# A two-block transformer kernel: the second block's head groups projected one ahead, masks and rotations on VectorE, meta rows padded

## The chip, the cores and the metric

The kernel runs on one core of one Trainium2 chip. The metric is the device time of one execution in microseconds (us); less is better. The core's engines are named as in the profile: PE is TensorE's matmul, PEld its weight load, DVE VectorE, ACT ScalarE, POOL GpSimd, SP SyncE, which issues most DMAs.

## The reference, cut to what matters

Two transformer blocks run one after the other on 256 tokens of width 1024, all in float32. The change touches only the mixer of the second block. It prepends 16 meta tokens (so 272 keys), and computes two attentions from one projection:

```python
u = rms_norm(h, pre_mix_gain)
qa, ka, va, qb, kb, vb, g = split(u @ w_in)   # qa: 16 heads of 64, ka/va: 4; qb/kb: 8 heads x 2 x 64; vb: 8 x 128
qa, ka, qb, kb = rope(...)
# windowed: key within +-128 positions, all meta keys, and a sink logit without a value
s = concat([where(mask, qa @ ka.T / 8, -1e30), qa @ ka_meta.T / 8, sink])
o_swa = softmax(s)[:, :-1] @ concat([va, va_meta])
# differential: dense over all 272 keys
o_diff = rms_norm((softmax(q1 k1) - lam * softmax(q2 k2)) @ vb) * gain
merged = sigmoid(g1) * (o_swa @ w_swa) + sigmoid(g2) * (o_diff @ w_diff)
```

## The kernel before

All weights are one stream of 128x1024 units (`next_unit`, L321; `fetch`, L287): SP fetches a unit by DMA (`raw`), ACT rounds it to fp32r (`hi`, two casts of 512 columns, L302), DVE forms the remainder (`lo`, two subtractions, L304). A float32 product is three fp32r matmuls (hi hi, hi lo, lo hi), so that one unit gives 24 matmuls of 256 or 272 columns (`mm_a`, L459). PE works through the units in stream order.

The mixer of the second block (from L924, 398 to 689 us of the trace with its neighbours) first projects values and the keys `ka`. The loop over `c` (four groups of four heads) projects the queries of its group (`q_ps`, two units), rotates them (`rope_T`, L492: ACT copies `raw` out of PSUM, tile name `t` in the profile; four DMAs on ACT's queue swap halves; DVE multiplies by the cosine, L512; `self.slow` multiplies by the sine, L513, and adds, L516), and stacks high and low parts (`stack_q`, L519: ACT rounds, `self.slow` subtracts, L526 and L527). `self.slow` is POOL here. Then `sink_attention` (L599) is called for two tiles of 128 queries (`qt`): for each of four heads a score tile in PSUM (two matmuls, and a third that adds the mask as a bf16 identity product, L566), and `sink_softmax`: DVE writes the sink logit into the score tile (L577) and takes the minimum (L571), ACT takes the exponential with its sum (L581), DVE the reciprocal (L583) and the scaling (L584). PE transposes the probabilities (`pt_ps`, L620), ACT and DVE split them into `pt` (L330, L331), and PE multiplies by the values (`o_ps`, L624); the third key tile is the 16 meta keys, and its matmuls contract over 16 rows. The first block uses `sink_softmax1` instead, with the mask and minimum in one DVE instruction.

The loop over `pr` (four pairs of differential heads) projects keys and queries of its pair, and for each head: scores, softmax, the difference `a` (L1013), its transposes (`at_ps`, `atm_ps`), and `od_ps`: for each `qt` two matmuls over 128 keys (L1032, L1033) and one over the 16 meta keys (L1034). Behind it comes a norm: ACT squares (`y`, L1038), DVE `ms` (L1040), POOL a power (`rq`, L1042), DVE scales (`y`, L1044), PE transposes (`ot_ps`, L1048), ACT and DVE split into `od_t`. The gates (`gate_ps`) and the two branch projections (`bs_ps` from `os_t`, `bd_ps` from `od_t`) follow.

The order of each engine is not that of the source: a scheduler picks among the instructions whose inputs it thinks ready, by priority, and puts projections between the steps of the attention. PSUM has few banks: projections (`acc`) rotate over two, the score tiles over three while the windowed attention runs, and `o_ps`/`od_ps` have one. A projection's bank comes free when ACT has copied it out.

## Time and profile before

| | |
|---|---|
| median of 3 runs | 908.08 us (905.95 to 909.29) |
| profiled execution | 907.98 us |
| its span, first to last instruction | 906.2 us |
| mean granted clock of TensorE | 0.994 of full speed |
| PE busy | 885.2 us, 98% of the span |
| DVE, ACT, POOL busy | 69%, 58%, 17% |
| the mixer's stretch, 398 to 689 us | PE busy 285.73 of 291 us |

The span is what the trace holds; 1.8 us of the execution's time lie outside of it. An engine's busy time counts the time in which at least one of its instructions runs. Matmuls overlap: one takes longer than the distance to the next one's start, so costs on PE are read from starts.

### The profile page before, as it was taken

How to read it: one execution, taken by the hardware profiler on the slowest of the kernel's cores; microseconds unless marked ns; L12 is line 12 of the kernel's file. 1: busy time of each engine (PE TensorE's matmuls, PEld its weight loads, DVE VectorE, ACT ScalarE, POOL GpSimd, SP SyncE). 2: the span in 40 equal slices, each digit the busy share in tenths (PEclk: the TensorE clock that was granted, in tenths of full speed). 3: DMA queues.
4: the chain of work that ended last, by engine and by line, in shares of the span. 5: the costliest groups of instructions: out<-in, count | busy, mean ns of one | idle time of the engine just before them, and what ended most of it. 6: DMA issues, size and time to landing. Idle time of an engine off the chain costs nothing. (4 is left out here: it accounts for less than half of the span.)

```text
span 906.2 us, 16452 instructions
## 1 busy us (share of the span) xinstructions
PE 885.2 (98%) x6172; PEld 814.2 (90%) x6172; DVE 626.4 (69%) x1203; ACT 522.1 (58%) x1145; POOL 150.4 (17%) x171
## 2 busy tenths in 40 slices
PE   6999999999999999999989999999999999999997
PEld 5899999998899999978978889899998799999996
DVE  5567698768655555665699999987566675656654
ACT  4643389546654444565658788876455554444542
POOL 2001110110001111110464535450110100000000
PEclk9999999999999999999989999999999999999999
DMA  8665754468476666654654344434467566666651
GB/s 296 223 204 178 200 165 149 151 206 310 163 215 197 187 190 186 204 192 153 179 171 113 110 119 132 133 91 135 140 186 237 183 216 202 187 186 187 187 162 46
DMA packets 48320, 160.25 MB, mean 177 GB/s; under 512 B 6497, under 2 KB 8417, under 8 KB 48242
## 3 DMA queue, kind: packets, MB, share of 16 engines
q1 hardware_dynamic: 43378, 153.49, 54.2%
q10 hardware_dynamic: 4672, 5.20, 2.1%
q8 instruction: 48, 0.79, 0.4%
q0 software_dynamic: 192, 0.52, 0.2%
q14 instruction: 30, 0.25, 0.1%
HBM read 151.38 MB, written 2.10 MB: 169 GB/s over the span
## 5 line engine op out<-in xcount | busy, mean ns | idle before, releaser
L304 DVE TENSOR_TENSOR lo<-raw,hi 128x512 fp32r<-128x512 f32 x536 | 373.7, 738 | 187.1 <-ACT hi L302 182.0
L302 ACT CAST hi<-raw 128x512 fp32r<-128x512 f32 x532 | 302.0, 618 | 231.3 <-issue 81.7
L471 PE MATMUL op<-hi,hid 128*128 128x512 f32 x416 | 128.9, 390 | 0.0
L459 PE MATMUL fi_ps<-xf2t,hi 128*128 128x256 f32 x640 | 114.4, 281 | 0.0
L459 PEld LDWEIGHTS fi_ps<-xf2t,hi 128*128 128x128 f32 x640 | 99.0, 188 | 0.9
L459 PE MATMUL fi_ps<-xf2t,lo 128*128 128x256 f32 x320 | 90.1, 281 | 0.0
L471 PEld LDWEIGHTS op<-hi,hid 128*128 128x128 f32 x416 | 76.3, 188 | 14.7
L471 PE MATMUL op<-lo,hid 128*128 128x512 f32 x208 | 81.1, 392 | 0.0
L459 PE MATMUL f_ps<-xf1t,hi 128*128 128x256 f32 x448 | 80.5, 281 | 0.0
L459 PEld LDWEIGHTS f_ps<-xf1t,hi 128*128 128x128 f32 x448 | 69.9, 188 | 1.2
L459 PE MATMUL f_ps<-xf1t,lo 128*128 128x256 f32 x224 | 63.0, 281 | 0.0
L459 PEld LDWEIGHTS fi_ps<-xf2t,lo 128*128 128x128 f32 x320 | 60.6, 189 | 0.0
L459 PE MATMUL q_ps<-x2t,hi 128*128 128x256 f32 x256 | 52.0, 294 | 0.0
L459 PE MATMUL gate_ps<-x2t,hi 128*128 128x256 f32 x256 | 48.7, 285 | 0.0
L459 PE MATMUL gate_ps<-x1t,hi 128*128 128x256 f32 x256 | 47.1, 283 | 0.0
L471 PEld LDWEIGHTS op<-lo,hid 128*128 128x128 f32 x208 | 39.0, 188 | 8.6
L459 PEld LDWEIGHTS q_ps<-x2t,hi 128*128 128x128 f32 x256 | 41.9, 195 | 0.8 <-issue 0.5
L459 PEld LDWEIGHTS f_ps<-xf1t,lo 128*128 128x128 f32 x224 | 42.4, 189 | 0.1
L853 POOL TENSOR_TENSOR sq<-relu 128x512 f32<-128x512 f32 x14 | 15.9, 1133 | 150.4 <-ACT relu L850 150.4
L459 PEld LDWEIGHTS gate_ps<-x2t,hi 128*128 128x128 f32 x256 | 39.9, 189 | 0.6 <-issue 0.5
L459 PEld LDWEIGHTS gate_ps<-x1t,hi 128*128 128x128 f32 x256 | 39.6, 189 | 0.2
L419 POOL TENSOR_SCALAR e<-ss 128x1 f32<-128x1 f32 (+1 forms) x11 | 3.0, 276 | 220.4 <-ACT py L1087 191.9
(321 smaller groups left out, 2004.0 us busy)
## 6 DMA issues: line engine op xcount, KB each, us to landing
raw<-in_wstream_dram SPq DMA_DIRECT2D x272, 512.0 KB, 4.1
sw<-t ACTq DMA_DIRECT2D x40, 64.0 KB, 4.1
x<-in_x_dram SPq DMA_DIRECT2D x3, 512.0 KB, 5.9
sw<-t ACTq DMA_DIRECT2D x40, 34.0 KB, 2.5
sw<-t ACTq DMA_DIRECT2D x8, 128.0 KB, 3.7
g_pre<-in_gains_dram SPq DMA_DIRECT2D x2, 512.0 KB, 6.5
x<-hf SPq DMA_DIRECT2D x2, 512.0 KB, 2.6
x<-x SPq DMA_DIRECT2D x2, 512.0 KB, 7.4
```

The lines of the kernel that those rows point to most:

```text
L302: nc.scalar.copy(hi[:, c:c + PIECE], raw[:, c:c + PIECE])
L304: nc.vector.tensor_sub(lo[:, c:c + PIECE], raw[:, c:c + PIECE], hi[:, c:c + PIECE].bitcast(F32))
L419: nc.gpsimd.tensor_scalar(out=e[:np_], in0=ss[:np_, 0:1], scalar1=1.0 / D, scalar2=EPS, op0=ALU.mult, op1=ALU.add)
L459: nc.tensor.matmul(out, wv[a][:, k, j * P:(j + 1) * P], XT[:, b, k, n0:n1], start=(i == 0), stop=(i == last))
L471: nc.tensor.matmul(out, XT[:, b, k0 + k, t0:t1], wv[a][:, k, c0:c0 + cn], start=(start and i == 0), stop=(stop and i == last))
L853: nc.gpsimd.tensor_tensor(out=q, in0=r, in1=r, op=ALU.mult)
```

## The change

Six edits in the second block, with the order of the weight stream changed to match:

- The queries of group `c + 1` are projected before the attention of group `c`; in the last group the first pair's keys and queries; the same for the pairs.
- `self.slow` is no longer POOL in this block: rotation and low query parts run on DVE.
- The mask matmuls are gone. A float32 table `masks2` (128 x 544) holds both masks; one DVE instruction reads the score tile, adds the mask, and takes the minimum with the sink, as in the first block. It writes to SBUF (`pn`); the exponential runs in place there, and the scaling is a copy with a scale on ACT. POOL copies the sink column.
- The output tile is combined through two ACT copies of 64x256 (first block's form) instead of one of 64x512.
- `vm` and two `atm` tiles have 128 rows, zero but for 16, so that `od_ps`'s third matmul contracts over 128 rows. `o_ps`'s meta matmuls still contract over 16.
- `ks` and `kl` have eight buffers instead of six; the value copies `vt` use `kl`'s.

```diff
-    "b2": dict(vt=4, sw=2, t1=2, t2=2, ks=6, kl=6, qe=2, qo=2, p=6, a=2, at=1, atm=2, y=1, pn=2, pt=2),
+    "b2": dict(sw=2, t1=2, t2=2, ks=8, kl=8, qe=2, qo=2, p=6, a=2, at=1, atm=2, y=1, pn=2, pt=2),
...
-    def scores(self, out, q, k, k0, k1, mask=None):
+    def scores(self, out, q, k, k0, k1):
...
-        nc.tensor.matmul(out, q, k[1][:, k0:k1], start=False, stop=(mask is None))
-        for i, (mi, c0) in enumerate(mask or ()):
-            nc.tensor.matmul(out[:, c0:c0 + P], self.identb, self.masks[:, mi * P:(mi + 1) * P],
-                             start=False, stop=(i == len(mask) - 1))
+        nc.tensor.matmul(out, q, k[1][:, k0:k1], start=False, stop=True)
...
-    def sink_softmax(self, s, n, nsink, out):
-
-        nc = self.nc
-        nc.vector.tensor_copy(s[:, n:n + 1], nsink)
-        nm = self.row_min(s)
-        p = self.t([P, NKEY + 2], "p")
-        den = self.sm(1, "den")
-        nc.scalar.activation(out=p[:, :n + 1], in_=s, func=AF.Exp, bias=nm, scale=-1.0, accum_out=den)
-        rc = self.sm(1, "rc")
-        nc.vector.reciprocal(rc, den)
-        nc.vector.tensor_scalar(out=out, in0=p[:, :n], scalar1=rc, scalar2=None, op0=ALU.mult)
-
-    def sink_softmax1(self, s, n, mask, nsink, p):
+    def sink_softmax(self, s, n, mask, nsink, p):
...
-        if isinstance(masks, list):
-            pn = self.t([P, 4, n], "pn")
...
+        pn = self.t([P, 4, n + 1], "pn")
+        nc.gpsimd.tensor_copy(pn[:, :, n], sink[:, 4 * c:4 * c + 4])
+        for h in range(4):
+            s = self.sbank([P, n], "s")
+            self.scores(s, q[h % 2][:, h // 2, qt * P:(qt + 1) * P], kst, 0, n)
+            self.sink_softmax(s, n, mask, sink[:, 4 * c + h:4 * c + h + 1], pn[:, h, :])
...
-        self.slow = nc.gpsimd
         rope_b = self.load("rope_b", [P, 2 * NKEY])
+        mk = self.load("masks2", [P, 2 * NKEY], rp)
...
-        vm = self.t([NMETA, D], "vm")
+
+        vm = self.t([P, D], "vm")
+        nc.gpsimd.memset(vm, 0.0)
+        atms = [self.t([P, NTOK], "atm") for _ in range(2)]
+        for t in atms:
+            nc.gpsimd.memset(t, 0.0)
...
+        qn = queries()
         for c in range(4):
-            q = self.stack_q(self.rope_T(self.proj_a(XT, name="q_ps"), 2, NTOK, rope_b, 32, scale=-0.125))
+
+            q = qn
+            if c < 3:
+                qn = queries()
+            else:
+                kn = keys()
+                qn = queries()
...
         for pr in range(4):
-            kb = keys()
-            q = self.stack_q(self.rope_T(self.proj_a(XT, name="q_ps"), 2, NTOK, rope_b, 32, scale=-0.125))
+            kb, q = kn, qn
+            if pr < 3:
+                kn = keys()
+                qn = queries()
...
-                atm = self.t([NMETA, NTOK], "atm")
-                nc.scalar.copy(atm, b[:NMETA])
+                atm = atms[m]
+                nc.scalar.copy(atm[:NMETA], b[:NMETA])
```

What the scheduler makes of it is seen in the engines' orders. A number behind a tile's name tells its instances apart; a row begins with the line, which is some lines off between the two kernels.

DVE ahead of the first score tile of the first group, before (`lo147` belongs to weight unit 147, and so on; `s_5080` is the first score tile):

```order
L304 TENSOR_TENSOR lo147_5861<-raw147_5862,hi147_5860 128x512 x2
L304 TENSOR_TENSOR lo148_5896<-raw148_5897,hi148_5895 128x512 x2
L304 TENSOR_TENSOR lo149_5949<-raw149_5950,hi149_5948 128x512 x2
L512 TENSOR_TENSOR t1_5591<-t2_5592,rope_b_4683 128x512
L304 TENSOR_TENSOR lo150_5981<-raw150_5982,hi150_5980 128x512 x2
L577 COPY s_5080<-nsink_347 128x1
L577 COPY s_5106<-nsink_347 128x1
L571 TENSOR_REDUCE mn_5085<-s_5080 128x1
```

And the same place of the changed kernel, where `s_5164` is the first score tile, and `masks2` and `nsink` are read by the one instruction:

```order
L314 TENSOR_TENSOR lo147_5808<-raw147_5809,hi147_5807 128x512
L529 TENSOR_TENSOR qe_5074<-t1_5064,qe_5074 64x512
L530 TENSOR_TENSOR qo_5075<-t1_5064,qo_5075 64x512
L314 TENSOR_TENSOR lo148_5843<-raw148_5844,hi148_5842 128x512
L519 TENSOR_TENSOR t1_5146<-t1_5146,sw_5145 128x512
L314 TENSOR_TENSOR lo148_5843<-raw148_5844,hi148_5842 128x512
L314 TENSOR_TENSOR lo149_5878<-raw149_5879,hi149_5877 128x512
L515 TENSOR_TENSOR t1_5388<-t2_5389,rope_b_4677 128x512
L579 ISA pn_5162,mn_5167<-s_5164,masks2_4679,nsink_341 128x272
```

The first score tile's DVE work stood behind unit 150's remainder and stands behind unit 149's now; the query's low parts (`qe`, `qo`) and sine steps (L519), which POOL held, stand among the remainders.

PE of the changed kernel at the end of the stretch in which the last two groups' attention runs. `s_6522` and `s_6529` are scores of the first differential head, `o_ps_5768` the second tile of group 2, `q_ps_6838` the queries of the second pair:

```order
L605 MATMUL o_ps_5768<-pt_5774,va_4798 128x512 x2
L605 MATMUL o_ps_5768<-pt_5784,va_4798 128x512 x2
L566 MATMUL s_6522<-ks_6014,qo_6153 128x272
L567 MATMUL s_6522<-kl_6015,qo_6153 128x272
L933 MATMUL vT_ps_5952<-ident_93,vt_5839 128x128
L933 MATMUL vT_ps_5952<-ident_93,vt_5874 128x128
L933 MATMUL vT_ps_5952<-ident_93,vt_5909 128x128
L933 MATMUL vT_ps_5952<-ident_93,vt_5944 128x128
L566 MATMUL s_6529<-ks_6008,qe_6152 128x272
L567 MATMUL s_6529<-kl_6009,qe_6152 128x272
L605 MATMUL o_ps_5768<-pt_5794,va_4798 128x512
L462 MATMUL q_ps_6838<-x2t_2567,hi162_6783 128x256 x2
```

ACT of the changed kernel for the same stretch (`pn_6238` are the probabilities of group 3's second tile; `pt_5794` goes into the last `o_ps_5768` above; the copy of `k_ps_6726` frees the bank that `q_ps_6838` takes):

```order
L582 ACTIVATE pn_6238,den_6265<-pn_6238,mn_6263 128x273
L340 CAST os_t_4884<-of_5719 128x2x128
L585 ACTIVATE pn_6238<-pn_6238,rc_6247 128x272
L972 COPY vm_4682<-vT_ps_5946 16x512
L582 ACTIVATE pn_6238,den_6275<-pn_6238,mn_6273 128x273
L585 ACTIVATE pn_6238<-pn_6238,rc_6257 128x272
L990 ACTIVATE p_6520,den0_6513<-s_6515,mn_6518 128x272
L585 ACTIVATE pn_6238<-pn_6238,rc_6267 128x272
L340 CAST pt_5794<-pt_ps_5789 16x512
L509 COPY t2_6761<-k_ps_6726 128x272
```

Scores, transposes and value products stand here without a projection between them on PE, and the next projection stands behind them; on ACT the copy that lets it begin is the last row.

PE before, behind the last differential head's `od_ps`, where the transposes of its normed output (`ot_ps_7776`) stand between gate projections, 38 matmuls of them behind `od_ps`:

```order
L459 MATMUL gate_ps_8118<-x2t_2573,lo183_8120 128x256
L459 MATMUL gate_ps_8118<-x2t_2573,hi183_8119 128x256 x2
L459 MATMUL gate_ps_8118<-x2t_2573,lo183_8120 128x256
L1048 MATMUL ot_ps_7776<-ident_93,y_7766 128x128
L459 MATMUL gate_ps_8118<-x2t_2573,hi183_8119 128x256
L1048 MATMUL ot_ps_7776<-ident_93,y_7766 128x128
L459 MATMUL gate_ps_8118<-x2t_2573,hi183_8119 128x256
L459 MATMUL gate_ps_8118<-x2t_2573,lo183_8120 128x256
```

And PE of the changed kernel at the last two heads (`od_ps_7664` is the last one, `ot_ps_7608` and `ot_ps_7681` the transposes of the last two heads' normed outputs):

```order
L462 MATMUL bd_ps_8090<-od_t_6318,hi184_8056 128x256 x2
L462 MATMUL bd_ps_8090<-od_t_6318,lo184_8057 128x256
L1040 MATMUL ot_ps_7608<-ident_93,y_7598 128x128 x2
L1024 MATMUL od_ps_7664<-vb_4681,at_7658 128x128
L1025 MATMUL od_ps_7664<-vb_4681,at_7658 128x128
L1026 MATMUL od_ps_7664<-vm_4682,atm_4685 128x128
L1024 MATMUL od_ps_7664<-vb_4681,at_7658 128x128
L1025 MATMUL od_ps_7664<-vb_4681,at_7658 128x128
L1026 MATMUL od_ps_7664<-vm_4682,atm_4685 128x128
L462 MATMUL bd_ps_8090<-od_t_6318,hi184_8056 128x256 x2
L462 MATMUL bd_ps_8090<-od_t_6318,lo184_8057 128x256
L1040 MATMUL ot_ps_7681<-ident_93,y_7671 128x128 x2
```

The gates stand ahead of these heads now, and three matmuls of `bd_ps` lie between the last `od_ps` and its `ot_ps`.

## Rows read from the trace of the kernel before

**Rows 1.** The page, part 1: each engine's busy us, share of the span, instructions.

```profile
PE 885.2 (98%) x6172; PEld 814.2 (90%) x6172; DVE 626.4 (69%) x1203; ACT 522.1 (58%) x1145; POOL 150.4 (17%) x171
```

**Rows 2.** Windows: stretch, length, busy us of PE, PEld, DVE, ACT, POOL; clock.

```profile
457.00:476.00 19.00, 15.91 (x100) 14.94 (x101) 17.52 (x34) 10.24 (x28) 10.29 (x7) 0.82 0.52 166
...
550.00:575.00 25.00, 24.86 (x192) 23.07 (x191) 23.44 (x46) 21.53 (x53) 13.54 (x13) 1.00 0.46 141
...
sum 291.00, PE 285.73 PEld 262.81 DVE 232.96 ACT 197.56 POOL 100.15; mean PE 25.98 PEld 23.89 DVE 21.18 ACT 17.96 POOL 9.10
```

**Rows 3.** Waits of PE from 398 to 689 us: total, times, longest.

```profile
PE s L563 <- ACT p L581: 2.9, 2, 2.2
```

**Rows 4.** Windows of two stretches in which PE idles.

```profile
105.00:115.00 10.00, 8.52 (x72) 8.31 (x71) 5.33 (x11) 4.38 (x9) 2.68 (x5) 1.00 0.90 224
468.80:475.70 6.90, 6.32 (x29) 6.08 (x30) 5.72 (x22) 4.09 (x14) 0.00 (x0) 0.51 0.58 183
```

**Rows 5.** PE's timeline, three places: start us, us, line, operation, count.

```profile
482.12 0.63 PE L624 MATMUL o_ps<-pt,va 128*128 128x512 f32 x2
482.58 0.60 PE L620 MATMUL pt_ps<-ident,pn 128*16 128x128 f32 x4
...
506.30 0.23 PE L566 MATMUL s<-masksb,identb 128*128 128x128 bf16 x1
506.33 0.48 PE L624 MATMUL o_ps<-pt,va 128*128 128x512 f32 x1
...
582.61 0.49 PE L1020 MATMUL at_ps<-ident,a 128*128 128x128 f32 x3
582.93 0.27 PE L1025 MATMUL atm_ps<-ident,a 128*16 128x128 f32 x1
...
583.29 0.38 PE L1032 MATMUL od_ps<-vb,at 128*128 128x128 f32 x2
...
584.88 0.48 PE L1034 MATMUL od_ps<-vm,atm 16*128 16x128 f32 x2
585.30 0.39 PE L564 MATMUL s<-kl,qe 128*128 128x272 f32 x1
585.53 0.29 PE L563 MATMUL s<-ks,qo 128*128 128x272 f32 x1
585.65 0.29 PE L564 MATMUL s<-kl,qo 128*128 128x272 f32 x1
```

**Rows 6.** The weights' lo subtraction, 398 to 689 us: ns least/median/most.

```profile
L304 DVE TENSOR_TENSOR lo<-raw,hi x136: 670/685/1819, 398.3 to 686.7; 128x512 fp32r<-128x512 f32 x136
```

**Rows 7.** Groups of instructions, 398 to 689 us: busy us, mean ns.

```profile
L304 DVE TENSOR_TENSOR lo<-raw,hi 128x512 fp32r<-128x512 f32 x136 | 110.0, 845 | 24.1 <-ACT hi L302 24.0
...
L584 DVE TENSOR_SCALAR pn<-p,rc 128x272 f32<-128x272 f32 x32 | 14.3, 476 | 0.2
...
L571 DVE TENSOR_REDUCE mn<-s 128x1 f32<-128x273 f32 x32 | 13.2, 429 | 0.1
```

**Rows 8.** Groups of the first block's attention: busy us, mean ns.

```profile
L597 ACT ACTIVATE pn<-pn,rc 128x256 f32<-128x256 f32 x8 | 3.9, 505 | 0.1
L591 DVE CUSTOM_DVE_ANT_0 pn<-s,masks,nsink 128x256 f32<-128x256 f32 x8 | 3.7, 479 | 0.0
...
L635 ACT COPY of<-o_ps 64x256 f32<-64x256 f32 x8 | 2.9, 369 | 1.6 <-PE o_ps L624 1.0 <-DVE of L636 0.5
```

**Rows 9.** ACT's timeline at 592 us: start us, us, line, operation.

```profile
592.40 0.49 ACT L998 ACTIVATE p<-s,mn 128x272 f32<-128x272 f32 x1
...
592.88 0.58 ACT L1022 COPY at<-at_ps 128x512 f32<-128x512 f32 x1
593.35 0.29 ACT L1038 ACTIVATE y<-od_ps 128x128 f32<-128x128 f32 x1
```

**Rows 10.** Timeline behind the last head's od_ps, 643 to 645.5 us.

```profile
643.08 0.28 ACT L1038 ACTIVATE y<-od_ps 128x128 f32<-128x128 f32 x1 [1.35 <-PE od_ps L1034]
...
644.71 0.61 DVE L1044 SCALAR_TENSOR_TENSOR y<-od_ps,rq,rows 128x128 f32<-128x128 f32 x2 [0.80 <-POOL rq L1042]
```

More of the change, by code (lines that the diff above doesn't have):

```diff
@@ L119, in pack_weights, with kq @@
     in_a(w_in2, o_ka)
+    def kq(p):
+        in_a(w_in2, o_kb + 256 * p)
+        in_a(w_in2, o_qb + 256 * p)
+    in_a(w_in2, o_qa)
     for c in range(4):
-        in_a(w_in2, o_qa + 256 * c)
+        if c < 3:
+            in_a(w_in2, o_qa + 256 * (c + 1))
+        else:
+            kq(0)
         if c == VB1:
@@ L183, in make_consts @@
     j = np.arange(P)[None, :]
-    add("masks", np.concatenate([np.where(j <= i, 0.0, MASKED), np.where(j >= i, 0.0, MASKED)], axis=1))
-    add("masks1", np.concatenate([np.where(j > i, 0.0, MASKED), np.where(j <= i, 0.0, MASKED)], axis=1))
+    le, ge, gt = (np.where(c, 0.0, MASKED) for c in (j <= i, j >= i, j > i))
+    z = np.zeros((P, P))
+    add("masks1", np.concatenate([gt, le], axis=1))
+    add("masks2", np.concatenate([z, le, z[:, :NMETA], ge, z, z[:, :NMETA]], axis=1))
     f = _freqs(500000.0, 16)
@@ L366, in consts2 @@
         cc = _CC
-        mk = self.wp.tile([P, UC], F32, tag="raw", bufs=4, name="mk")[:, 0:2 * P]
-        a, n = cc["masks"]
-        nc.sync.dma_start(out=mk, in_=io["consts"][:, a:a + n])
-        self.identb = cp.tile([P, P], BF16, name="identb")
-        self.masks = cp.tile([P, 2 * P], BF16, name="masksb")
-        nc.gpsimd.tensor_copy(self.identb, self.ident)
-        nc.gpsimd.tensor_copy(self.masks, mk)
         self.vec = cp.tile([P, 48], F32, name="vec")
@@ L597, in sink_softmax1, with sink_attention @@
         nc.scalar.activation(out=p[:, :n], in_=p[:, :n], func=AF.Copy, scale=rc)
-    def sink_attention(self, q, kst, vs, sink, ktiles, masks, OT, c, qt):
+    def sink_attention(self, q, kst, vs, sink, ktiles, mask, OT, c, qt):
         nc = self.nc
         n = ktiles[-1][0] + ktiles[-1][1]
-        if isinstance(masks, list):
-            pn = self.t([P, 4, n], "pn")
-            for h in range(4):
-                s = self.sbank([P, n + 1], "s")
-                self.scores(s[:, :n], q[h % 2][:, h // 2, qt * P:(qt + 1) * P], kst, 0, n, masks)
-                self.sink_softmax(s, n, sink[:, 4 * c + h:4 * c + h + 1], pn[:, h, :])
-        else:
-            pn = self.t([P, 4, n + 1], "pn")
-            nc.gpsimd.tensor_copy(pn[:, :, n], sink[:, 4 * c:4 * c + 4])
-            for h in range(4):
-                s = self.sbank([P, n], "s")
-                self.scores(s, q[h % 2][:, h // 2, qt * P:(qt + 1) * P], kst, 0, n)
-                self.sink_softmax1(s, n, masks, sink[:, 4 * c + h:4 * c + h + 1], pn[:, h, :])
+        pn = self.t([P, 4, n + 1], "pn")
[4 more added lines that the diff above has]
+            self.sink_softmax(s, n, mask, sink[:, 4 * c + h:4 * c + h + 1], pn[:, h, :])
         o = self.pv([P, 4, P], "o_ps")
@@ L626, in sink_attention @@
         of = self.t([P, 2, P], "of")
-        if isinstance(masks, list):
-            ol = self.t([64, 4, P], "ol")
-            nc.scalar.copy(ol, o[64:128])
-            for e in range(2):
-                nc.vector.tensor_add(of[64 * e:64 * e + 64], o[0:64, e:4:2], ol[:, e:4:2])
-        else:
-            for e in range(2):
-                r = slice(64 * e, 64 * e + 64)
-                nc.scalar.copy(of[r], o[64:128, e:4:2])
-                nc.vector.tensor_add(of[r], o[0:64, e:4:2], of[r])
+        for e in range(2):
+            r = slice(64 * e, 64 * e + 64)
+            nc.scalar.copy(of[r], o[64:128, e:4:2])
+            nc.vector.tensor_add(of[r], o[0:64, e:4:2], of[r])
         ts = slice(qt * P, (qt + 1) * P)
@@ L969, in keys, with queries @@
             return r
+        def queries():
+            return self.stack_q(self.rope_T(self.proj_a(XT, name="q_ps"), 2, NTOK, rope_b, 32, scale=-0.125))
         OS = self.big("C", 8, "os_t", NKEY)
@@ L974, in block2 @@
         ka = keys()
+        qn = queries()
         for c in range(4):
-            q = self.stack_q(self.rope_T(self.proj_a(XT, name="q_ps"), 2, NTOK, rope_b, 32, scale=-0.125))
+            q = qn
+            if c < 3:
+                qn = queries()
+            else:
+                kn = keys()
+                qn = queries()
             for qt in range(2):
-                self.sink_attention(q, ka[c], va, self.nsink[:, 8:24], kts, [(0, P)] if qt == 0 else [(1, 0)],
-                                    OS, c, qt)
+                self.sink_attention(q, ka[c], va, self.nsink[:, 8:24], kts, mk[qt], OS, c, qt)
             if c == VB1:
                 for i, b in v_T(4, "vb_ps"):
-                    nc.scalar.copy(vall[i][:, 512:1024], b.rearrange("p m d -> p (m d)"))
+                    nc.scalar.copy(vall[i][:b.shape[0], 512:1024], b.rearrange("p m d -> p (m d)"))
         OD = self.big("A", 8, "od_t", NKEY)
```

10 lines of the change are left out of this document (5 added, 5 removed).

## The prediction

> **What bounds the kernel now.** I read the page first: PE is busy for 98% of the span [rows 1], so time comes only from PE's own work, its few idle stretches, or its clock. The windows of the mixer tell where these lie: over its 291 us PE is idle for 5.3 us, and 3.1 of them lie in 457 to 476 us, where the granted clock is 0.82 [rows 2]; 2.2 us are left for everything else. The list of waits names the largest: the score tiles wait 2.9 us in two waits for the exponential that should free their bank [rows 3]. The clock is at about half speed, the lower of its two levels, for 6.9 us right behind that [rows 4]. DVE is the neighbour to watch: 17.52 of 19 us in that window and 23.44 of 25 later, beside a POOL that works half of the time [rows 2]. The weights' subtractions show why: the same instruction takes 0.67 us at least and 1.82 at most [rows 6]; in the timeline the long ones lie over a running POOL instruction.
>
> **PE's own work.** Padding of the meta rows. In the timeline, a head's twelve `od_ps` matmuls take 2.01 us from the first start (583.29) to the next matmul's (585.30), which itself takes 0.39 us where the next one takes 0.29. Three 128-column transposes take 0.32 us to the next start, 0.107 each [rows 5], so twelve would take 1.28. The excess, 2.01 - 1.28 + 0.10 = 0.83 us, belongs to two visits to the 16-row matmul: 0.41 us each. Before there are 32 visits (8 heads with two `od_ps` each, 8 attention tiles with two `o_ps` each); the changed order has 14, all `o_ps`, two pairs of which became neighbours. 18 x 0.41 = 7.4 us less.
>
> The masks: the 32 matmuls seem to take 0.23 us each, but the next one starts 0.03 us behind [rows 5], so their removal saves 32 x 0.03 = 1.0 us. PE's work: **-8.4 us**.
>
> By the Trainium skill the first of these would be nothing. Its page "TensorE: Matmul & The Clock Gate" prices a matmul by its columns alone ("Back-to-back issue gap"), and says in "LDWEIGHTS" that a load with fewer rows takes the same time as a full one; the page "TensorEngine Tiling (Array Packing)" says, under its tiling modes, that changing the mode drains the engine, which is what the rows look like. The trace sides with the second: 0.41 us for a visit. The first is a rival below.
>
> **The start of the windowed attention.** Before, the query's steps go through POOL, and the first scores' minimum stands on DVE behind `lo150`, in a stretch where those subtractions are at their longest. The changed order has it behind `lo149`, with the query projected earlier, and the only POOL instructions left there are keys'. The moved work costs DVE 16 steps of 512 columns in rotations and 16 in `stack_q` at 0.685 us [rows 6], and 20 steps of 272 columns at 0.43 (the reduction of that width [rows 7]): 30.5 us. It gets back 32 x (0.48 + 0.43 + 0.15) us of scaling, minimum and sink copy (0.15, an estimate for one column; the reciprocal's stay) against 32 x 0.58 for the joint instruction (0.48 for 256 columns [rows 8], an estimate of 0.50 for 272 and 0.08 for its read): 15 us. The other 15 us are more than covered if the 136 subtractions fall from 0.845 us on average [rows 7] towards their median of 0.685 [rows 6], which is 22 us. So DVE ends with less, and the waits of this start go: **-3.1 us** of idle, and **-3.1 us** of clock (6.32 busy us at 0.51 [rows 4] are 3.2 at full speed). Of the 2.2 us of idle elsewhere I take two thirds, since some of it stands just ahead of the same place: **-1.4 us**. If the cover fails, these three are nothing. Up to here: 907.98 - 8.4 - 3.1 - 3.1 - 1.4 = 892.0 us. The profiled execution lies 0.1 us from the median, so no correction.
>
> **What it adds: ACT.** 32 scalings move to ACT at about 0.5 us [rows 8], and 16 copies at 0.37 [rows 8] replace 8 of about 0.58 (as the 512-column copy [rows 9]): +16 + 5.9 - 4.7 = 17 us as they are listed; ACT starts the next instruction some 0.1 us before the last has ended (592.88 + 0.58 against 593.35 [rows 9]), so nearer 13. They fall into the 90 us of the windowed attention, where ACT is already 86% busy at the end (21.53 of 25 [rows 2]).
>
> What decides is the order. Since projections now run a group ahead, the attention of groups 2 and 3 comes late and packed. From behind the last score of group 2's second tile to the first `q_ps_6838`, PE has 24 `k_ps` and 22 score matmuls (0.13 us each, for starts 0.12 apart), 32 transposes (0.11), 17 `o_ps` (0.23: 0.46 for two [rows 5]) and three 16-row visits (0.41): 6.0 + 3.5 + 3.9 + 1.2 = 14.6 us. In the same stretch ACT has 11 scalings (0.41), 9 exponentials (0.48 from start to start [rows 9]), 7 casts of `pt` (0.47), 2 `hi` (0.52), 4 copies of `of` (0.27), 4 `ks` and 3 `os_t` (0.35), 2 copies for rotations and one of `vm` (1.25 together); what has no row goes by rows of like size less 0.1. That is 4.5 + 4.3 + 3.3 + 1.0 + 1.1 + 2.5 + 1.3 = 18 us, and its last row is what frees `q_ps_6838`'s bank. PE must wait at least the difference, 3.4 us; with hand-overs from DVE on the way (a minimum, a reciprocal for each head), or if ACT comes late into the stretch, up to 8. Nothing is queued on PE that could go ahead. I take **+5 us**.
>
> **What it adds: the last heads.** The gates that hid the last norms stand earlier now. From the first square to the second scaled `y` take 643.08 to 645.32, 2.24 us [rows 10], through ACT, DVE, POOL and DVE. Behind `od_ps_7591` PE has 6 transposes and 3 `bd_ps` (1.0 us) to hide it, behind `od_ps_7664` 3 `bd_ps` (0.35), and the next `bd_ps` also needs the split of `ot_ps` (two steps, about 1 us): 1.2 + 1.9 + 1.0, **+4 us**; bounds 0, if ACT is done early with the first, and 5.
>
> **The clock.** Idling of 2.9 us within 5 us was followed by 6.9 us at the lower level; idling of 1.5 us within 10 was not [rows 4]. The two new stalls are of the first sort or between. A drop costs 3.1 us where PE is the bound. Two chances of a quarter each: +1.5 us. The new table is a DMA that is not waited for, and the zeroing is POOL's, early. Sum: 892.0 + 5 + 4 + 1.5 = **902.5 us**, 0.6% less.
>
> **The rivals.** What a measurement can tell from no change is about 0.5%, 4.5 us.
>
> *A, the forecast* (0.50): the gain of 16 us, eaten by half by the packed stretch and the last heads; 897 to 908 us, below 903.5 in two cases of three.
>
> *B, the new stalls stay away* (0.20): ACT's list in the packed stretch is worked off in time because the scores' exponentials start earlier than I assume, and the last norms are hidden. For it: in the first block the same softmax runs beside projections without a listed wait. Against: there are no projections here. 889 to 897 us.
>
> *C, slower* (0.13): ACT becomes the bound of the whole windowed attention, not of one stretch. Its 20 to 21.5 us of each 25 rise by 13 to 17 us over 90, to 24 to 26. At 24 it keeps up, from 25 on PE waits for every tile: 5 to 8 us more over the four groups, and a clock drop or two on it (3 to 6 us): 902.5 + 10 = 913 us, 910 to 918.
>
> *D, the padding buys nothing* (0.09): the time is that of the columns, and the distances I read come from something else, such as the small loads' position; then only the two visits fewer of `o_ps` count, 0.8 us, and the sum is 6.6 us higher: 909 us. This is what the Trainium skill's page "TensorE: Matmul & The Clock Gate" (the sections above) would make of it. Against it: the 16-row matmuls are the only ones in the row of twelve that are late.
>
> *E, the start stays as it is* (0.08): DVE's 30 us of moved work hold the first scores up as POOL did. 3.1 + 3.1 come back, and the forecast's sum is 909 us.
>
> **How the numbers follow.** Faster by over 0.5% (below 903.5): 0.33 of A and all of B, and a little of D and E, 0.55. Slower (above 912.6): most of C, some of D and E, 0.14. The rest, 0.31, is the same. The range takes in B's middle and D, E and the lower part of C: 891 to 911 us.
>
> **What would show it.** `od_ps` L1034's successor must take its place without excess, twelve matmuls in 1.3 us. The wait of scores for the exponential near 466 us and the lower clock behind it must be gone; `lo` must average below 0.75 us. PE must show waits for ACT of 3 to 8 us in all where groups 2 and 3 are attended to, with ACT above 95% there, and 3 to 5 us around the last two `ot_ps`. I am wrong if PE idles less than 3 us in both (B), if ACT is above 95% from the first group on (C), or if the twelve take 2 us still (D).

## The result, and the profile after

The changed kernel takes 911.62 us (median of 14 runs, 909.21 to 914.79), the kernel before 908.0 (14 runs, 904.67 to 911.76): a ratio of 1.0051, with a 95% interval of 1.0039 to 1.0063. It is slower by half a per cent; the forecast was 902.5 us and faster. The profiled execution is the slowest of the 14: 914.79 us, with a span of 913.0 where before it was 906.2.

The page, part 1, of the changed kernel, answers to [rows 1]:

```profile
PE 884.4 (97%) x6140; PEld 815.0 (89%) x6140; DVE 618.4 (68%) x1223; ACT 535.6 (59%) x1185; POOL 86.5 (9%) x128
```

PE is busy for as long as before, though it has 32 matmuls less and two thirds of the 16-row ones are gone, and the span is 6.8 us longer. So the saved work came back as something else. The windows of the changed kernel's mixer (stretch, its length, busy time of PE, PEld, DVE, ACT, POOL, granted clock, DMA share, GB/s) answer to [rows 2]:

```profile
457.00:476.00 19.00, 18.26 (x143) 17.88 (x143) 18.71 (x47) 16.21 (x42) 0.00 (x0) 1.00 0.67 202
476.00:500.00 24.00, 22.34 (x173) 20.83 (x171) 18.75 (x52) 20.30 (x52) 2.25 (x4) 1.00 0.50 155
500.00:525.00 25.00, 23.46 (x157) 20.99 (x158) 18.04 (x42) 19.29 (x46) 0.49 (x1) 0.93 0.43 138
525.00:550.00 25.00, 20.20 (x92) 14.62 (x91) 18.77 (x61) 21.19 (x57) 2.10 (x5) 0.80 0.18 54
550.00:575.00 25.00, 24.51 (x179) 21.64 (x179) 21.36 (x47) 20.48 (x52) 5.94 (x6) 1.00 0.21 64
650.00:660.00 10.00, 6.61 (x39) 5.99 (x40) 3.52 (x9) 3.46 (x11) 1.21 (x2) 0.83 0.02 6
```

Length less PE's busy time is its idle time. At 457 to 476, where before 3.09 us were idle at a clock of 0.82, 0.74 are left at full clock. But 476 to 575 now has 8.49 us of idle time (0.94 before), most of it at 525 to 550, where PE ran 92 matmuls instead of 184, and 650 to 660 has 3.39 (none before). Over 25 us no other engine is full: where PE idles most, ACT has 21.19 us and DVE 18.77. In slices of 2 us it looks different (same columns):

```profile
516.00:518.00 2.00, 1.33 (x6) 0.81 (x6) 2.00 (x8) 2.00 (x5) 0.00 (x0) 1.00 0.75 250
522.00:524.00 2.00, 2.00 (x13) 1.85 (x13) 0.40 (x1) 0.23 (x1) 0.00 (x0) 0.83 0.07 27
530.00:532.00 2.00, 0.94 (x3) 0.18 (x2) 1.92 (x7) 1.98 (x5) 0.00 (x0) 1.00 0.00 0
536.00:538.00 2.00, 2.00 (x17) 1.91 (x17) 0.49 (x2) 0.31 (x1) 0.07 (x1) 0.91 0.23 57
540.00:542.00 2.00, 1.31 (x8) 0.86 (x6) 2.00 (x6) 1.98 (x7) 0.00 (x0) 1.00 0.00 0
542.00:544.00 2.00, 1.08 (x4) 0.42 (x4) 1.84 (x8) 1.99 (x6) 0.00 (x0) 0.79 0.47 117
```

In the slices shown in which PE idles, ACT and DVE are both full, mostly with the steps of the softmax; where PE is full with projections (522 to 524, 536 to 538), both stand nearly still. From 476 to 560 us there are eleven slices of 2 us in which PE idles for more than 0.25 us, 8.0 us in all: in each of them DVE or ACT is busy for 93% or more, in six of them both for over 90%. So softmax and projections come in turns here instead of side by side.

A table of windows over exactly the stretches at the lower clock:

```profile
519.30:522.70 3.40, 3.40 (x17) 3.40 (x17) 2.13 (x5) 2.50 (x7) 0.00 (x0) 0.50 0.70 238
532.90:536.30 3.40, 3.40 (x16) 3.19 (x15) 1.40 (x3) 3.03 (x8) 0.00 (x0) 0.50 0.23 58
543.20:550.00 6.80, 6.07 (x20) 3.99 (x21) 4.92 (x18) 5.70 (x16) 0.95 (x2) 0.50 0.20 72
655.80:659.20 3.40, 3.13 (x13) 2.96 (x14) 1.72 (x3) 2.10 (x5) 0.00 (x0) 0.50 0.00 0
sum 17.00, PE 16.00 PEld 13.54 DVE 10.17 ACT 13.33 POOL 0.95; mean PE 4.00 PEld 3.38 DVE 2.54 ACT 3.33 POOL 0.24
```

Sixteen busy us at half speed cost 8 us, where before 6.32 [rows 4] cost 3.2. The mixer (from 398 us on, to 689 before and 695.8 now) is 297.8 us long, before 291.0; its idle time is 13.8 us, before 5.3. So +8.5 of idle time, +4.8 of clock, and PE's own work is what is left of +6.8: **-6.5 us** by busy times, an estimate that takes half of the busy time at half speed as the clock's.

PE's waits in the mixer (what waits, for whom: total us, times, longest; the first six of ten) show that the idle time has no single owner; [rows 3] is gone from the list:

```profile
PE ot_ps L1040 <- DVE y L1036: 3.1, 2, 1.9
PE s L566 <- DVE mn L579: 3.0, 5, 0.7
PE o_ps L605 <- DVE of L611: 2.1, 2, 1.7
PE o_ps L605 <- ACT pt L340: 1.9, 3, 0.9
PE o_ps L605 <- DVE pt L341: 1.1, 2, 0.9
PE s L566 <- DVE qe L529: 0.8, 1, 0.8
```

Hand-overs inside the windowed softmax and its output make most of it (the joint minimum, the transposed probabilities `pt`, the output half `of`), each below 2 us. PE's timeline in the worst stretch (start, duration, line; in brackets the idle time ahead) shows what stands between two of them:

```profile
540.34 0.29 PE L567 MATMUL s<-kl,qo 128*128 128x272 f32 x1
541.31 0.49 PE L605 MATMUL o_ps<-pt,va 16*128 16x512 f32 x1 [0.69 <-ACT pt L340]
541.73 0.40 PE L566 MATMUL s<-ks,qe 128*128 128x272 f32 x1
541.96 0.28 PE L567 MATMUL s<-kl,qe 128*128 128x272 f32 x1
543.17 0.79 PE L605 MATMUL o_ps<-pt,va 16*128 16x512 f32 x1 [0.92 <-DVE pt L341]
```

Between two `o_ps` that wait there are two score matmuls, 0.23 us from start to start, and no projection: PE waits for steps of ACT and DVE, which are both full here (540 to 544 us above), and has nothing to put over it.

### The profile page after: what moved, and what is told of

Same layout as the page of the kernel before. It is cut to its first block, busy times and chain, and to the rows that moved or that the text cites. A ratio compares the mean times of both kernels' runs of the same rounds, so it can differ in the third digit from the quotient of the medians.

```text
span 913.0 us, 16364 instructions
## 1 busy us (share of the span) xinstructions
PE 884.4 (97%) x6140; PEld 815.0 (89%) x6140; DVE 618.4 (68%) x1223; ACT 535.6 (59%) x1185; POOL 86.5 (9%) x128
## 4 chain that ended last, share of the span: by engine, by line
PE 31%; ACT 7%; DVE 7%; DMA 3%; issue 2%; ACTq 1%; POOL 0%; SPq 0%; DVEq 0%; POOLq 0%
PE fi_ps L462 12%; PE op L474 6%; DVE lo L314 3%; PE gate_ps L462 2%; ACT hi L312 2%; PE bd_ps L462 2%; PE bs_ps L462 2%; DMA sw<-t 2%; DMA raw<-in_wstream_dram 2%; PE k_ps L462 1%; ACT pn L582 1%; ACT pn L585 1%; PE fi_ps L484 1%; DVE pn L579 1%; DVE pt L341 1%
## 5 line engine op out<-in xcount | busy, mean ns | idle before, releaser
L314 DVE TENSOR_TENSOR lo<-raw,hi 128x512 fp32r<-128x512 f32 x536 | 356.8, 705 | 183.8 <-ACT hi L312 178.0
L462 PE MATMUL q_ps<-x2t,hi 128*128 128x256 f32 x256 | 46.9, 282 | 0.0
L462 PEld LDWEIGHTS q_ps<-x2t,hi 128*128 128x128 f32 x256 | 39.6, 188 | 0.3 <-ACT t L509 0.2
L462 PE MATMUL gate_ps<-x1t,lo 128*128 128x256 f32 x128 | 36.2, 283 | 0.0
L462 PE MATMUL q_ps<-x2t,lo 128*128 128x256 f32 x128 | 36.1, 282 | 0.0
```

Of the source, the lines that this page charges most:

```text
L314: nc.vector.tensor_sub(lo[:, c:c + PIECE], raw[:, c:c + PIECE], hi[:, c:c + PIECE].bitcast(F32))
L462: nc.tensor.matmul(out, wv[a][:, k, j * P:(j + 1) * P], XT[:, b, k, n0:n1], start=(i == 0), stop=(i == last))
```

## The experiments

All compute the whole reference. The expectations speak of theories: that projecting ahead makes the attention late and packed (O, the forecast's cause); that ACT's scalings are too much (S), or the steps moved to DVE (V); that shorter steps let the scheduler spread the projections unevenly over the tiles (P); that any edit redraws the order, so the place of a few projections is luck (R); that the buffers or ACT's work around the softmax hold it up (W); and that the scheduler has a wrong idea of how long the joint instruction takes (K). Q, J and L are the rivals named beside them. Since the idle time stands mainly in 440 to 560 us, each kernel is shown by that window (columns as above). The kernel before and the changed one:

```profile
440.00:560.00 120.00, 115.40 (x855) 105.86 (x853) 112.34 (x252) 90.44 (x218) 59.41 (x48) 0.97 0.45 131
```

```profile
440.00:560.00 120.00, 109.95 (x765) 98.64 (x764) 95.08 (x236) 97.54 (x240) 11.33 (x18) 0.94 0.43 130
```

They idle for 4.6 and 10.05 us.

### Projecting ahead: taken back, and alone

`e1_not_ahead` is the changed kernel with the old order of the stream and loops:

```diff
     for p in range(4):
-        if p < 3:
-            kq(p + 1)
+        in_a(w_in2, o_kb + 256 * p)
+        in_a(w_in2, o_qb + 256 * p)
...
-            kb, q = kn, qn
-            if pr < 3:
-                kn = keys()
-                qn = queries()
+            kb = keys()
+            q = queries()
```

> The changed kernel with the projections back in the old order: each group's and each pair's own queries and keys are projected right before its attention, and the weight stream is in that order; all else as changed. Theory O (projecting one ahead takes the cover from the last groups' attention and from the last heads, where PE then waits for a chain over three engines): the waits of 498 to 553 us and around the last two ot_ps go, and of the lowered clock with them; PE's own work stays 8 us shorter than before: 895 to 901 us. Theory S (the scalings and copies moved to ACT make ACT the bound of the windowed attention, whatever the order): the waits stay, 907 to 912 us. Theory V (the steps moved to DVE do it): the same as S.

`e2_ahead_alone` is the kernel before with just these lines the other way round, and the buffers `ks` and `kl` at 8.

> The kernel before with only the projections one ahead (stream order, loops, and the buffers of ks, kl and vt that this needs); masks, softmax, POOL and the 16-row matmuls as before. Theory O: slower than before, 912 to 922 us, with PE's waits between the last groups' scores and values and around the last two ot_ps. Theories S and V: 904 to 908 us, since ACT and DVE have nothing more to do and the first scores come with more distance to their query.

The first took 912.12 us, 1.0070 [1.0042, 1.0098] of before: nothing is given back. Its window and that of the second (910.46 us, 1.0044 [1.0030, 1.0058]):

```profile
440.00:560.00 120.00, 111.78 (x811) 102.71 (x811) 99.39 (x242) 101.50 (x248) 13.61 (x18) 0.96 0.43 138
```

```profile
440.00:560.00 120.00, 113.22 (x826) 102.04 (x826) 113.30 (x247) 87.02 (x214) 55.40 (x47) 0.97 0.42 131
```

Idle for 8.2 us without projecting ahead, 6.8 with it alone. It costs something by itself, though no more than an order drawn anew does below, but the changed kernel's stalls stay when it is taken out: over the whole mixer (398 to 700 us) PE idles for 15.0 us in `e1_not_ahead`, 13.8 in the changed kernel, 5.3 in the one before. The forecast's cause falls.

### ACT's scalings on DVE

`e3_scale_dve` changes one line of the changed kernel:

```diff
-        nc.scalar.activation(out=p[:, :n], in_=p[:, :n], func=AF.Copy, scale=rc)
+        if n == NKEY:
+            nc.vector.tensor_scalar(out=p[:, :n], in0=p[:, :n], scalar1=rc, scalar2=None, op0=ALU.mult)
+        else:
+            nc.scalar.activation(out=p[:, :n], in_=p[:, :n], func=AF.Copy, scale=rc)
```

> The changed kernel with the scaling of the windowed probabilities on DVE again (in place); ACT has 32 instructions of 0.51 us fewer. Theory O: 909 to 913 us, a chain of the same length over the same engines. Theory S: 900 to 905 us, the waits of 498 to 553 us largely gone. Theory V: slower, 914 us or more.

909.6 us, 1.0036 [1.0022, 1.0050]: 1.4 us better than the changed kernel by the ratios, whose intervals overlap. In its window ACT has 92.0 us instead of 97.5, DVE 112.2 instead of 95.1, and PE still idles for 7.9. ACT's load is a part at most: what is taken from one full engine goes to the other.

### One edit at a time on the kernel before

`e4_pad_alone` pads the meta rows and does nothing else:

```diff
-        vm = self.t([NMETA, D], "vm")
+        vm = self.t([P, D], "vm")
+        nc.gpsimd.memset(vm, 0.0)
+        atms = [self.t([P, NTOK], "atm") for _ in range(2)]
...
-                atm = self.t([NMETA, NTOK], "atm")
-                nc.scalar.copy(atm, b[:NMETA])
+                atm = atms[m]
+                nc.scalar.copy(atm[:NMETA], b[:NMETA])
```

> The kernel before with only the zero-padded meta rows of the differential heads. By the excess read in the trace (16 visits to the 16-row matmul at 0.41 us): 6.6 us less, 901.5 us, 900 to 903. If the time were that of the columns alone: 908 us.

904.07 us (12 runs, 901.43 to 909.59), 0.9978 [0.9959, 0.9997]: the lowest median of all, but 2.4 us less than before where 6.6 were expected. PE's waits in the mixer of its profiled run, which took 901.84 us:

```profile
PE s L563 <- ACT p L581: 2.9, 2, 2.2
PE at_ps L1024 <- DVE a L1017: 1.4, 2, 0.8
...
PE ot_ps L1052 <- DVE y L1048: 0.8, 1, 0.8
```

The first row is that of before, word for word [rows 3]. The next two were not in before's list: matmuls that have become shorter cover less of DVE's steps for a head, so a part of the padding's gain turns into waits (7.5 us of idle time from 398 to 700 us, where before has 5.3). That does not explain the median: the execution profiled is 6.1 us below the one profiled before, nearly what was expected, and one of the fastest of the twelve. No trace shows what the slower ones lose.

`e5_slow_dve_alone` leaves out `self.slow = nc.gpsimd`, so that rotations and low parts go to DVE.

> The kernel before with only the rotations and low query parts on DVE instead of POOL. Theory P (each step made shorter lets the scheduler put the late attention tiles close together and the last heads behind the projections; PE then waits there, whichever engine does the work): in this order 28 and 0 projection matmuls stand ahead of the sixth and seventh tile's value products (64 and 79 before), and 3 between the last od_ps and its transposes (38 before), so 3 to 5 us of waits in the windowed attention and 4 to 5 at the last heads, against 4 to 6 gained at its start and from POOL: 906 to 912 us. Theory S (ACT's added work is what makes PE wait): ACT has nothing more to do, 900 to 904 us.

912.95 us, 1.0084 [1.0066, 1.0102]. Its order leaves only three `bd_ps` between the last head's `od_ps` and `ot_ps`, and PE waits 2.8 us in three waits for the last heads' `y`: the loss at the last heads comes with this edit, by way of the order. It needs no projecting ahead (`e1_not_ahead` waits 4.1 us there), and it is not this edit's alone: `n2_before_vb3` below, which changes no work, has 1.4 us of it. In the window `e5_slow_dve_alone` idles for only 4.3 us.

`e6_softmax_alone` has the changed kernel's windowed softmax, scalings and output copies in the kernel before:

```diff
-        nc.vector.tensor_copy(s[:, n:n + 1], nsink)
-        nm = self.row_min(s)
...
+        nc.vector.tensor_tensor_reduce(out=p[:, :n], in0=s, in1=mask, scale=1.0, scalar=nsink, op0=ALU.add,
+                                       op1=ALU.min, accum_out=nm)
...
-        nc.vector.tensor_scalar(out=out, in0=p[:, :n], scalar1=rc, scalar2=None, op0=ALU.mult)
+        nc.scalar.activation(out=p[:, :n], in_=p[:, :n], func=AF.Copy, scale=rc)
```

> The kernel before with only the new softmax (mask and minimum in one DVE instruction, no mask matmuls, scaling and output copies on ACT in the first block's form). Theory P: 13 and 0 projection matmuls ahead of the fifth and sixth tile, so 4 to 7 us of waits between 500 and 555 us, none at the last heads, which keep 29 and 11 matmuls of cover: 906 to 911 us. Theory S: the waits are spread over all eight tiles, 908 to 914 us.

915.43 us, 1.0121 [1.0100, 1.0142], and its window idles for 11.6 us, more than the changed kernel's:

```profile
440.00:560.00 120.00, 108.39 (x760) 96.77 (x759) 92.52 (x204) 96.71 (x236) 52.30 (x46) 0.96 0.39 120
```

The dearest of these edits is the softmax, by itself +9.4 us in a kernel that projects nothing ahead. Alone, the edits come to +4.0, +6.9, +9.4 and -2.4 us on their own references, 18 together, where the whole change costs 3.6: they don't add.

### Where the projections stand, and how much is luck

`e7_vb1` is the changed kernel with another place for half a value projection, which spreads the projections more evenly over the tiles; `e8_vb1_gates` also projects all four second gates ahead of the `bd_ps`, to cover the last heads.

```diff
-VB1 = 2
+VB1 = 1
```

> The changed kernel with the other half of the value projection (four units) one group earlier in the stream and the source. All instructions are the same; the projections between the eight windowed tiles become 120, 42, 78, 53, 67, 76, 101 instead of 80, 96, 24, 24, 0, 64, 135. Theory P: the waits of 498 to 553 us and their lowered clock fall from 17 us to under 5, the last heads' 4 us stay: 899 to 904 us. Theory S: 908 to 913 us, since ACT's work is the same.

> As the last, and all four second gates projected ahead of the four branch projections of the differential heads, so that 21 gate matmuls stand behind the second last od_ps and none behind the last. Theory P: of the last heads' 4.1 us of waits some 2 stay: 2 us less than the kernel of the last run, 897 to 902 us. If those waits are not from the missing cover, no difference to it.

914.88 us, 1.0093 [1.0074, 1.0112], and 916.66 us, 1.0122 [1.0102, 1.0143]; both slower than the changed kernel, where 897 to 904 were expected. By the order of their instructions, 80, 96, 24, 24, 0, 64 and 135 projection matmuls stand ahead of the last seven tiles' `o_ps` in the changed kernel, 120, 42, 78, 53, 67, 76 and 101 in `e7_vb1`; in the window it idles for 9.1 us all the same. An even spread is not enough.

The same switch in the kernel before (`n1_before_vb1`: 1; `n2_before_vb3`: 3), in the changed kernel (`x_vb3`: 3), and two buffer counts in the kernel before (`n3_before_bufs`: `ks` and `kl` at 8, `vt` with `kl`'s tag) measure what an edit costs that changes no work at all:

> The kernel before, all instructions the same, with the other half of the value projection one group earlier in the stream and source, so that only the scheduler's order is drawn anew. Theory R (the order of the kernel before fits the chip by selection; any edit that makes the scheduler draw a new one costs 5 to 12 us of waits and clock, and this, not the edits' work, is what the change loses): 910 to 917 us, with 12 us or more of waits where before has 6.6. Rival Q (the waits come with the edits themselves, since they shorten DVE's steps or load ACT): 904 to 908 us.

> As the last, with that half one group later. Here 3 to 5 projection matmuls stand behind the last heads' od_ps instead of 38. Theory R: 910 to 917 us, 4 of it at the last heads. Rival Q: 904 to 909 us.

> The changed kernel, all instructions the same, with the other half of the value projection one group later; 48, 81, 90 and 105 projection matmuls stand ahead of the last four tiles' value products, 22, 26 and 0 ahead of the second to fourth. Theory R: another draw, anywhere from 903 to 917 us, and more than 3 us from the changed kernel's 911.6. Rival Q: 909 to 914 us.

> The kernel before with only the change's buffer counts (eight ks and kl, the value copies in kl's buffers). The order is the same as before up to the gates in the middle of the windowed attention and differs behind them. Theory R: 908 to 914 us. Rival Q: 904 to 907 us.

Before: 909.07 us, 1.0025 [1.0009, 1.0041]; 913.63, 1.0082 [1.0057, 1.0106]; buffers 908.89, 1.0015 [1.0001, 1.0030]. The changed kernel: 911.26, 1.0047 [1.0029, 1.0065], as without. Every such edit made the kernel before slower, by 1.6 to 6.3 us in the median, so a part of what any edit costs here is the new order. Yet none of these three idles as long in the window as the kernels with the new softmax: 7.4, 6.3 and 3.8 us.

### What in the softmax

`f4_soft_pbuf` is `e6_softmax_alone` with the joint instruction and the exponential on the six buffers `p` that they had before, so that `pn` is not held from the first step on; `f7_joint` also gives the scaling back to DVE and the output copies back as they were, so that of the softmax edit only the joint instruction is left, without the mask matmuls, and 32 sink copies on POOL:

```diff
+        w = p
+        if n == NKEY:
+            w = self.t([P, NKEY + 2], "p")[:, :n + 1]
+            nc.gpsimd.tensor_copy(w[:, n:n + 1], nsink)
...
+        if n == NKEY:
+            nc.vector.tensor_scalar(out=p[:, :n], in0=w[:, :n], scalar1=rc, scalar2=None, op0=ALU.mult)
```

> The new softmax alone (915.4 us), but with the joint instruction and the exponential in the six buffers of p and the scaling on ACT from there into pn, so that pn is held for its last step only. If holding pn costs the waits: 2 to 5 us between 475 and 560 us, 906 to 910 us. If the scaling and copies on ACT do: still 8 us or more there, 912 to 917 us.

> The kernel before with only the joint instruction for mask and minimum and no mask matmuls: it writes to the six buffers of p that the exponential used before, the exponential runs in place there, DVE scales into pn, POOL copies the sink's column, and the output tile is combined as before. Theory W (the waits of the new softmax come from the probabilities' tile pn, which is now held from the first step of its tile, and from the scaling and copies on ACT, not from the joint instruction): 1 to 4 us of waits between 475 and 560 us, 904 to 908 us. Rival J (a shorter first step of the softmax alone lets the scheduler pack the tiles): 8 us or more of waits there, 911 to 917 us.

916.4 us, 1.0093 [1.0078, 1.0109], with 9.0 us of idle time in the window, so the buffers are a part at most; and 925.04 us, 1.0180 [1.0161, 1.0199], the slowest of all. In `f7_joint`'s window ACT and DVE are less busy than in the kernel before, and PE idles for 10.2 us:

```profile
440.00:560.00 120.00, 109.82 (x774) 100.39 (x773) 105.71 (x241) 84.91 (x206) 56.75 (x65) 0.94 0.44 130
```

That is 5.6 us more than before, a third of the 17 that it loses. Over the whole mixer (398 to 700 us) it idles for 16.4 us, 11.1 more, and the lower clock costs some 8 us more than before, an estimate from the granted clock of 2-us slices.

`f3_pad_joint` is `f7_joint` with the padding, `f2_pbuf_dve_pool` the changed kernel with these buffers, scaling on DVE and rotations on POOL:

> As the last, with the zero-padded meta rows. Theory W: 2 to 6 us less than the last, 900 to 905 us, the fastest so far. Rival J: 906 to 914 us.

> The changed kernel with three things undone: the joint instruction writes to the buffers of p, DVE scales into pn, and rotations and low query parts are on POOL again. What is left is projecting ahead, the padding, the joint instruction and the output copies. Theory W: waits between 475 and 560 us at 2 to 5 us instead of 11.4, the last heads' 4 us stay: 903 to 908 us. If projecting ahead is what packs the tiles after all: 8 us or more there, 909 to 914 us.

916.8 us, 1.0097 [1.0080, 1.0114], and 914.87, 1.0076 [1.0060, 1.0092]. Padding is worth 8.2 us there.

`g1_split_joint` divides the changed kernel's joint instruction into an addition and a minimum, which is more work on DVE and gives the scheduler another estimate; `g2_old_softmax` is the changed kernel with the whole softmax of before (mask matmuls, minimum, scaling on DVE, output copies), with projecting ahead, rotations on DVE and padding kept:

```diff
+            nc.vector.tensor_tensor(out=p[:, :n], in0=s, in1=mask, op=ALU.add)
+            nm = self.row_min(p)
```

> The changed kernel with the joint DVE instruction split into two ordinary ones (the mask added from PSUM into pn, then the minimum over pn with the sink's column): DVE has 32 instructions of some 0.4 us more on the way from each score tile to its exponential. Theory K (the scheduler, which sets the order by its own idea of durations, takes the joint instruction for shorter than the chip does, so that its orders come apart from the chip's timing): although the work is more, the waits between 475 and 560 us fall from 11.4 to 5 us or less, 903 to 909 us. Rival L (the waits are those of a long chain over busy engines): they grow with the added work, 913 us or more.

> The changed kernel with the softmax of the kernel before (mask matmuls, sink copy, minimum, exponential from PSUM, scaling on DVE, old output copies); projecting ahead, rotations on DVE and the padding stay. If the new softmax is what brings the waits of 475 to 560 us whatever stands beside it: 1 to 5 us of them instead of 11.4, the last heads' 4 us stay, 901 to 906 us. If the whole of the edits does it: 8 us or more, 909 us or more.

918.67 us, 1.0112 [1.0092, 1.0131]: some 5.5 us slower than with one instruction by the ratios, so that it is one is not the fault. And 906.95 us, 0.9984 [0.9964, 1.0004], 12 runs: all of the loss is gone, though PE's idle time is not down to before's (9.4 us in the mixer against 5.3). Its window:

```profile
440.00:560.00 120.00, 113.19 (x832) 102.47 (x831) 108.90 (x277) 86.67 (x209) 10.64 (x12) 0.97 0.43 130
```

6.8 us of idle time instead of 10.05. Over all kernels this divides them without overlap: with the mask added on DVE, jointly or in two steps, the window idles for 7.9 to 11.7 us (12 kernels), with the old softmax for 3.8 to 7.4 (8 kernels), whatever else is changed. The window was chosen with the results known, and the gap in it is 0.5 us; but over the whole mixer, 398 to 700 us, the same two groups idle for 12.6 to 16.9 and for 5.3 to 10.1 us. This division carries the argument more than the one time of `g2_old_softmax`, since an edit without any work moved the kernel before by as much. And it is one of idle time, not of the total: `e5_slow_dve_alone` and `n2_before_vb3`, with the old softmax, take at least as long as the changed kernel.

## Why the prediction was wrong

Two terms failed: the clock's, which was forecast as at most two drops, at a quarter each, and came as four, and the idle time of the windowed attention, which was counted in one stretch and put down to projecting ahead. The terms in their order:

**PE's own work (-8.4): right in cause, nearly in size.** The twelve matmuls of a head in PE's timeline, beside [rows 5]:

```profile
602.55 0.46 PE L1024 MATMUL od_ps<-vb,at 128*128 128x128 f32 x2 [0.21 <-DVE of L611]
602.85 0.39 PE L1025 MATMUL od_ps<-vb,at 128*128 128x128 f32 x2
603.08 0.39 PE L1026 MATMUL od_ps<-vm,atm 128*128 128x128 f32 x2
...
603.89 0.48 PE L462 MATMUL bs_ps<-os_t,hi 128*128 128x256 f32 x2
```

1.34 us from the first start to the next matmul's, where it was 2.01, against 1.3 forecast. The balance above gives -6.5 for all of PE's work; it may be too small, since waits that are shorter than the modelled length of the matmul before them count there as work. Rival D falls with this, and with `e4_pad_alone`. The Trainium skill's pricing of a matmul by its columns ("TensorE: Matmul & The Clock Gate", "Back-to-back issue gap") doesn't hold where one of 16 rows stands among those of 128: the row of twelve (2.01 us with such ones, 1.34 without) decides against it.

**The start (-3.1 idle, -3.1 clock): right.** 0.74 us of idle time are left of 3.09 and the clock there is 1.00; the 6.9 us at half speed are gone from that place. The cover that the prediction named is there: `lo` averages 719 ns, where it was 845 [rows 7] and had to fall below 750. Rival E falls.

**The -1.4 of other idle time: wrong in sign**, as part of the next.

**"I take +5 us" for the packed stretch: right in size for that stretch, wrong in cause, and wrong as the only place.** The stretch that the forecast lists (24 `k_ps`, 22 scores, up to the first `q_ps`) is 526.9 to 552.7 us in the trace. PE idles for 4.4 us in it, against 5; but it takes 25.8 us where the forecast's terms give 19.6, since 10.2 us of it ran at half speed. Ahead of it, from 476 us on, PE idles for some 4 us more, where it idled for 0.8 before and the forecast expected less still. So 476 to 575 us cost 8.49 us of idle time, 7.55 more than before, where the forecast's two terms, +5 and -1.4, make +3.6. The forecast's sign, ACT above 95%, fails over 25 us (85%) and holds in most of the slices in which PE idles; but DVE is as full there, and the forecast counted DVE only as hand-overs: of the waits listed in that stretch 1.9 us are for ACT and 2.5 for DVE. The cause that it gave was "projections now run a group ahead". With projecting ahead undone the loss stays (`e1_not_ahead`), with the old softmax it goes (`g2_old_softmax`), and the new softmax brings it without any projecting ahead (`e6_softmax_alone`). I had costed the new softmax as work taken from DVE (+18.6 against -33.9 us) and from PE, and never as a change of the chain and of the order that comes from it. The load was right and the waits were not: ACT's copy and scale averages 515 ns and the joint instruction 494, as estimated.

```profile
L314 DVE TENSOR_TENSOR lo<-raw,hi 128x512 fp32r<-128x512 f32 x137 | 94.1, 719 | 19.9 <-ACT hi L312 19.8
...
L579 DVE CUSTOM_DVE_ANT_0 pn<-s,masks,nsink 128x272 f32<-128x272 f32 x32 | 15.1, 494 | 4.0 <-PE pt_ps L601 3.2 <-PE s L567 0.6
...
L585 ACT ACTIVATE pn<-pn,rc 128x272 f32<-128x272 f32 x32 | 15.8, 515 | 0.1
```

(Groups of the mixer: line, operation, count, busy us, mean ns, idle time ahead and what ended it.) Rival C, slower, was right in sign and wrong in mechanism: ACT does not become the bound of the whole windowed attention (77 to 85% in the windows from 476 to 575 us), and taking 32 scalings from it gives back 1.4 us, not clear of noise.

**The last heads (+4): right in place and nearly in size.** 650 to 660 us idles for 3.39 us. The two waits for `y` take 1.2 and 1.87 us, against 1.2 and 1.9 forecast. The timeline around the second, behind the last `od_ps`:

```profile
652.93 0.28 ACT L1030 ACTIVATE y<-od_ps 128x128 f32<-128x128 f32 x1 [0.97 <-PE od_ps L1026]
...
653.89 0.69 POOL L1034 TENSOR_TENSOR rq<-ms,nhalf 128x2 f32<-128x2 f32 x1 [3.37 <-DVE ms L1032]
654.62 0.61 DVE L1036 SCALAR_TENSOR_TENSOR y<-od_ps,rq,rows 128x128 f32<-128x128 f32 x2 [0.87 <-POOL rq L1034]
...
655.12 0.50 PE L1040 MATMUL ot_ps<-ident,y 128*128 128x128 f32 x2 [1.87 <-DVE y L1036]
```

From square to the second scaled `y` it is 2.3 us, as worked out from [rows 10], and PE has three short `bd_ps` for it.

**The clock (+1.5): the step that failed by most.** Two chances of a quarter were given to one drop each. There were four stretches at half speed: one ahead of the packed stretch, two in it, one behind the last heads. They cost 8 us; so the clock went from a gain of 3.1 and a loss of 1.5 to a loss of 4.8 against before, 6.4 us worse than forecast.

The sum with what was measured: -6.5 of work, -2.4 at the start, +7.5 in 476 to 575, +3.4 at the last heads, +4.8 of clock, which is the +6.8 of the profiled mixer. The forecast's sum is -5.5: of the 12.3 us between them 6.4 are the clock, 4.0 idle time in all, and 1.9 PE's work. The median moved by 3.6; the profiled execution is the slowest of its kernel, so in a usual one some of these terms are smaller, and no trace shows which.

**What stays open** is why the mask on DVE orders the windowed attention worse. The step itself is hardly longer: 494 ns and a read of 80, against a minimum of 429 [rows 7] and the sink's copy. `f7_joint` changes little else and loses 17 us. Three things go with it and were not separated: the score's bank is freed by DVE's minimum instead of ACT's exponential, which changes when the scheduler may put the next scores; the 32 mask matmuls are no longer there; and `f7_joint` alone has 32 small POOL copies. How much is the mechanism and how much the draw of one order, of which null edits alone make up to 6.3 us, these runs can't say.

## What to carry to other kernels

Cost an edit in a scheduled kernel twice: by the load that it moves, and by the waits that it leaves PE with when nothing else is ready. A share of 85% over 25 us can hide slices in which the engine is full and PE idles, beside others in which it stands still: read such a stretch in slices of 2 us. Edits that each redraw the order don't add up, so take them one at a time and keep those that leave the order nearly alone: padding the few-row matmuls to full rows did (the sequences of ACT and DVE in the mixer's trace agree with before's to 98%), and that alone is a little faster than the kernel before (0.9978, interval up to 0.9997) and clearly faster than the changed one. Where an in-order engine takes over steps from an idle one, look at what they wait for: here DVE now stands still behind the rotation's DMA.

## What was not expected

DVE's waits from 475 to 560 us in the changed kernel:

```profile
DVE sw L516 <- DMA sw<-t: 6.8, 2, 3.4
DVE pn L579 <- PE pt_ps L601: 3.2, 3, 1.5
```

Two rotations hold the whole engine for 3.4 us each until their swapped halves have landed. PE was busy all through both (480.7 to 484.2 and 506.5 to 510 us), so no run shows that they cost time. In the kernel before, POOL waits 13.5 us for such DMAs from 440 to 560 us, and no wait of PE is put down to them.

The clock fell behind idle time that is spread out: at 525 to 550 us the longest wait of PE is the 0.92 us shown above, the idle time is 4.8 of 25 us, and the granted clock of that window is 0.80.

The time of one kernel spread by more than its profile explains: `e4_pad_alone` ran between 901.43 and 909.59 us, in 12 runs, at the same order of instructions.
